# The Fourier branch's output map on half of the positions, in an encoder block on one Trainium2 core

## The chip, the core and the metric

The kernel runs on one core of one Trainium2 chip. The metric is the device time of one execution in microseconds; before the change it is 1738.92 us, the median of 3 runs (1738.01 to 1740.28). Engines are named as the profile does: PE is TensorE, DVE VectorE, ACT ScalarE, POOL GpSimd, SP SyncE, which here issues nearly all DMAs, in the order of its own queue.

## The reference

One encoder layer on two batches: a sample of 1024 tokens and a prompt of 256, each with 16 meta tokens in front (1040 and 272 positions), model width 1024. What the change touches is branch A and the merge:

```python
def fourier_mix(f):
    fg = f.astype(jnp.float32).reshape(b, l, N_FOURIER_GROUPS, FOURIER_GROUP)
    y = jnp.real(jnp.fft.fftn(fg, axes=(1, 3), norm='ortho'))
    return y.reshape(b, l, FOURIER_WIDTH).astype(f.dtype)
...
    a = bidirectional_gqa(q, k, v) @ w_attn_o
    fo = fourier_mix(f) @ w_four_o
    merged = g_attn * a + g_four * fo
    x = x + merged @ w_out
```

f has 4 groups of 128 channels. The real part of the 2-D transform is a sum of two products: cosine over positions with cosine over channels, less sine with sine. Over the L positions the cosine part is even (position l and L - l have the same value) and the sine part is odd (opposite sign). Over the 128 channels of a group it is likewise, so channels 0 to 64 determine the rest.

## The kernel before

All matrix products run in three passes: each float32 operand is split into a high part (a cast to float32r) and a low part (the operand less its high part), and `three` (L213) issues high x high, high x low and low x high (L218, L219, L220). The tokens are in three chunks, `CH_N` = 512, 512 (sample) and 256 (prompt).

The stages: norms and transposed activations; the Fourier branch (`fourier`, L485) with part of the gate products beside it; queries and keys; attention, whose gaps on PE are filled with the gate products of chunks 1 and 2 (`gate_gen`, L425, drawn by a Filler); the merge (`merge`, L969), first chunk 0, then chunks 1 and 2; the output projection `w_out`; and the SwiGLU, the largest part.

`fourier` computes the channel products, then the position products: for the sample positions 1 to 520 (260 columns a half), for the prompt positions 16 to 271 (256 columns). The results come in five kinds of rows: even channels (2 tiles of 128 rows, 32 or 64 channels a group), odd channels (2 tiles), and the 4 rows of k = 64. For the sample the other positions are mirrored copies (L636, L639). `store` (L576) writes all of it to DRAM, `f_d`, for all 1280 tokens, 512 rows.

`load_af` (L938) fetches the attention output (two parts, added at L964) and the Fourier result of a chunk and splits both: 4 + 4 k tiles of 128 rows. `merge` goes over 8 units of 128 output columns. For each unit `load` (L973) fetches the weights (`w_m`: attention and even/odd Fourier rows; `w_mb`: the mirrored Fourier rows) and the two gates of the chunk; `need` (L988) adds and subtracts the mirrored rows (L992, L993), splits the 1024 columns (ACT L202, POOL L203), and takes the sigmoids. Then each chunk has 4 k tiles x 3 matmuls for the attention and as many for the Fourier half; DVE multiplies each with its gate (L1036, L1037), adds (L1038), and the sum is split into M (L1040, L1041). SP fetches two units ahead.

SBUF is a set of equal slots; a tile's slot comes free when its last reader is done. Within the attention, the order on PE, ACT and DVE is the program's; elsewhere a scheduler sets the order of each engine when the program is built, and an engine then works in that order. So a DMA that waits in SP's queue holds all later ones.

Of the kernel before, what the change touches and what calls it, by code (L numbers as in the profile page):

```python
# [17 lines left out]
P = 128  # L18
# [18 lines left out]
# pairs of token tiles of the SwiGLU's products: the first three with 384 columns, the others with 256  # L37
# [18 lines left out]
SLOT = 1056  # L56
N_SLOTS = 27
# [58 lines left out]
class Slot:  # L116
# [57 lines left out]
class Kernel:  # L174
    def __init__(self, tc, nc, a, o, pools):
# [18 lines left out]
        self.f_d = [self.dram.tile([512, n], F32, name=f"f_d{i}") for i, n in enumerate(CH_N)]  # L194

# [17 lines left out]
    def three(self, out, pairs, first=True, last=True):  # L213
        """out += hi.hi + hi.lo + lo.hi over pairs of ((stationary hi, lo), (moving hi, lo))."""
# [7 lines left out]
    def rstd(self, ss, n, scale, eps, name):  # L222
        """(ss * scale + eps) ** -0.5 for n sums a partition."""
# [7 lines left out]
    def norm(self, x, out, g, rows=P, name=""):  # L231
        """out = x * rsqrt(mean(x^2) + eps) (* g) along the columns."""
# [16 lines left out]
    # hT of chunk c: k pairs a slot (c0, c1), three k a slot (c2 with the meta tokens behind)  # L249
# [22 lines left out]
    def transpose_pair(self, hs, t, off, ps, name, tag="tr"):  # L272
        """Two token tiles (slots, 1024 columns) into hT columns off .. off+256."""
# [12 lines left out]
    def gained(self, t, ks, lo, hi, pt):  # L286
        """hT columns lo .. hi of some k tiles from the transposed rows, times the gains of their features."""
# [137 lines left out]
    def gate_gen(self, chunks, lo_engine):  # L425
        """Gate logits of the chunks; while there is a self.later, what is not for TensorE is put into it."""
# [57 lines left out]

    def fourier(self, ps):  # L485
        nc, a, sl = self.nc, self.a, self.sl
        # even and odd parts over positions n <-> L - n
# [26 lines left out]
        # channels: U[n, k] for every n tile, cos from the even part, sin from the odd part  # L514
# [34 lines left out]
        for j, m in enumerate((P, 9)):  # L549
            nc.gpsimd.dma_start(tp[j][:m, :1024], a["pos_p"][j, :m])  # L550
# [37 lines left out]
        # prompt: positions 16.. unfolded
        ms = [P, 9]
        for kind, p in kinds:  # L590
            rows = 4 if kind == "4" else P
            pf = ps.tile([P, 512], F32, tag="mm", name=f"fp{kind}{p}")
            tb = 512 if kind == "o" else 0
            self.three(
                pf[:rows, :256],
                [
                    (u_of(kind, p, up, j, m), (tp[j][:m, tb : tb + 256], tp[j][:m, tb + 256 : tb + 512]))
# [4 lines left out]
            nc.vector.tensor_copy(st[:rows, :256], pf[:rows, :256])  # L602
            store(kind, p, st, self.f_d[2], 0, 256, 2)
# [3 lines left out]
        # sample: positions l = 1..520, the others mirrored  # L607
# [9 lines left out]
        for i, (kind, p) in enumerate(kinds):  # L617
# [5 lines left out]
            for half in range(2):  # L623
# [9 lines left out]
                sgn = -1.0 if kind == "o" else 1.0  # L633
                if half == 0:
                    nc.vector.tensor_copy(st[:rows, 0:245], pf[:rows, 15:260])
                    nc.scalar.mul(st[:rows, 764:1024], pf[:rows, 259::-1], sgn)  # L636
                else:
# [3 lines left out]
            for c in range(2):  # L641
                store(kind, p, st, self.f_d[c], c * 512, (c + 1) * 512, c)
# [1081 lines left out]
```

## Time and profile before

| | before |
|---|---|
| median of 3 runs | 1738.92 us |
| span of the profiled execution (first to last instruction) | 1737.8 us |
| what lies around the span, by the median | 1.1 us |
| granted clock of PE, mean | 0.997 |
| attention ends (last product with the values) | about 663.7 us |
| the merge's matmuls | 670.9 to 787.6 us |
| output projection, first to last matmul | 787.6 to 904 us |

The profile gives busy time by engine, a chain of work that ended last, groups of instructions by line and tile, tables by stretch of time, and the instructions in order of time with what ended the idle time before each. Times are from the start of the span. A matmul's duration includes its way through the array, so that matmuls overlap; the distance between two starts is what each costs. In a row such as `m<-afl,ml 128*128 128x512`, m is the tile written, the next names are the tiles read (a slot may still bear an older name), then come the stationary and the moving operand's shapes.

### The profile page before, as it was taken

How to read it: one execution, taken by the hardware profiler on the slowest of the kernel's cores; microseconds unless marked ns; L12 is line 12 of the kernel's file. 1: busy time of each engine (PE TensorE's matmuls, PEld its weight loads, DVE VectorE, ACT ScalarE, POOL GpSimd, SP SyncE). 2: the span in 40 equal slices, each digit the busy share in tenths (PEclk: the TensorE clock that was granted, in tenths of full speed). 3: DMA queues.
4: the chain of work that ended last, by engine and by line, in shares of the span. 5: the costliest groups of instructions: out<-in, count | busy, mean ns of one | idle time of the engine just before them, and what ended most of it. 6: DMA issues, size and time to landing. Idle time of an engine off the chain costs nothing.

```text
span 1737.8 us, 25952 instructions
## 1 busy us (share of the span) xinstructions
PE 1697.8 (98%) x9917; PEld 1511.1 (87%) x9917; DVE 1140.9 (66%) x2084; ACT 720.6 (41%) x1391; POOL 239.6 (14%) x239
## 2 busy tenths in 40 slices
PE   7999999999999999999999999999999999999997
PEld 6888879878888888788879999999999998888886
DVE  5424544568777776963379766676666668765685
ACT  6323333456666666531355322222222234444444
POOL 3001333210100103423343000000000000000002
PEclk9999999999999999999999999999999999999999
DMA  5144331322222229735451222222232237553434
GB/s 190 63 149 162 116 116 55 122 74 67 70 61 59 61 79 352 250 119 170 145 182 64 85 82 95 90 96 89 94 98 84 71 126 255 198 182 101 159 97 153
DMA packets 100292, 212.06 MB, mean 122 GB/s; under 512 B 10373, under 2 KB 46877, under 8 KB 100168
## 3 DMA queue, kind: packets, MB, share of 16 engines
q1 hardware_dynamic: 90952, 192.98, 33.2%
q10 hardware_dynamic: 7824, 12.53, 2.0%
q0 software_dynamic: 1392, 4.90, 0.9%
q8 instruction: 78, 1.28, 0.3%
q14 instruction: 46, 0.38, 0.1%
HBM read 151.05 MB, written 59.31 MB: 121 GB/s over the span
## 4 chain that ended last, share of the span: by engine, by line
PE 67%; DVE 7%; DMA 3%; issue 3%; ACT 1%; POOL 1%; SPq 0%; POOLq 0%; DVEq 0%; ACTq 0%
PE i L218 9%; PE i L220 9%; PE i L219 9%; PE o L220 5%; PE o L219 5%; PE o L218 5%; PE S L898 4%; PE pt L832 4%; PE g L218 2%; PE pv L852 2%; PE g L219 2%; PE g L220 2%; PE pv L853 2%; PE wo L220 2%; PE wo L219 2%
## 5 line engine op out<-in xcount | busy, mean ns | idle before, releaser
L1227 ACT CAST w<-wi 128x512 fp32r<-128x512 f32 x168 | 104.0, 621 | 274.0 <-PE i L220 218.0
L218 PE MATMUL i<-A,w 128*128 128x384 f32 x616 | 208.4, 338 | 3.0 <-ACT w L1227 2.6
L220 PE MATMUL i<-A,w 128*128 128x384 f32 x616 | 208.1, 338 | 2.3 <-POOL w L1229 2.3
L219 PE MATMUL i<-A,w 128*128 128x384 f32 x616 | 207.9, 338 | 0.0
L218 PE MATMUL i<-Ah,w 128*128 128x256 f32 x616 | 173.0, 281 | 1.6 <-DVE sc L1283 1.5
L220 PE MATMUL i<-Ah,w 128*128 128x256 f32 x616 | 173.2, 281 | 0.0
L219 PE MATMUL i<-Al,w 128*128 128x256 f32 x616 | 172.9, 281 | 0.0
L834 ACT CAST pT<-pt 128x512 fp32r<-128x512 f32 x156 | 90.7, 582 | 97.1 <-PE pt L832 94.3
L835 DVE TENSOR_TENSOR pT<-pt,pT 128x512 fp32r<-128x512 f32 x156 | 106.9, 686 | 34.2 <-ACT pT L834 33.0
L1229 DVE TENSOR_TENSOR w<-wi,w 128x512 fp32r<-128x512 f32 x154 | 105.3, 685 | 28.7 <-ACT w L1227 28.3
L903 DVE TENSOR_REDUCE sm<-S 128x1 f32<-128x1040 f32 (+1 forms) x80 | 86.5, 1082 | 50.7 <-PE S L898 47.4
L218 PEld LDWEIGHTS i<-A,w 128*128 128x128 f32 x616 | 116.5, 189 | 3.6 <-ACT w L1227 2.9
L220 PEld LDWEIGHTS i<-A,w 128*128 128x128 f32 x616 | 116.4, 189 | 3.2 <-POOL w L1229 3.2
L218 PEld LDWEIGHTS i<-Ah,w 128*128 128x128 f32 x616 | 116.0, 188 | 2.2 <-DVE sc L1283 1.7
L219 PEld LDWEIGHTS i<-A,w 128*128 128x128 f32 x616 | 116.3, 189 | 0.0
L219 PEld LDWEIGHTS i<-Al,w 128*128 128x128 f32 x616 | 116.2, 189 | 0.0
L220 PEld LDWEIGHTS i<-Ah,w 128*128 128x128 f32 x616 | 116.0, 188 | 0.0
L227 POOL TENSOR_SCALAR fin0r<-fin0ss 128x1 f32<-128x1 f32 x1 | 0.8, 788 | 755.8 <-ACT X L235 755.8
L910 ACT ACTIVATE p<-S,sm 128x1040 f32<-128x1040 f32 (+1 forms) x80 | 80.2, 1003 | 33.6 <-DVE sm L903 27.0
L832 PE MATMUL pt<-ident,p 128*128 128x128 f32 (+1 forms) x624 | 93.4, 272 | 0.0
L220 PE MATMUL o<-wfo,act 128*128 128x512 f32 (+1 forms) x212 | 82.1, 388 | 2.1 <-DVE act L1361 2.1
L219 PE MATMUL o<-wfo,act 128*128 128x512 f32 (+1 forms) x212 | 81.9, 386 | 0.0
(745 smaller groups left out, 4475.9 us busy)
## 6 DMA issues: line engine op xcount, KB each, us to landing
wi<-w_fi SPq DMA_DIRECT2D x48, 512.0 KB
wg<-w_g SPq DMA_DIRECT2D x32, 512.0 KB
act_d<-sc SPq DMA_DIRECT2D x77, 192.0 KB
act<-act_d SPq DMA_DIRECT2D x37, 320.0 KB
wfo<-w_fo SPq DMA_DIRECT2D x21, 512.0 KB
X<-act_d SPq DMA_DIRECT2D x31, 320.0 KB
act_d<-sc SPq DMA_DIRECT2D x77, 128.0 KB
gate<-gs ACTq DMA_DIRECT2D x32, 256.0 KB
```

Of the source, the lines that this page charges most:

```text
L218: mm(out, sh, mh, start=first and i == 0, stop=False)
L219: mm(out, sh, ml, start=False, stop=False)
L220: mm(out, slo, mh, start=False, stop=last and i == n - 1)
L832: nc.tensor.transpose(pt[:rows, h * P : (h + 1) * P], me.ps4[h][:, col : col + rows], self.ident[:])
L834: nc.scalar.copy(pT[:rows, :512], pt[:rows, :])
L835: nc.vector.tensor_tensor(pT[:rows, 512:1024], pt[:rows, :], f32(pT[:rows, :512]), op=ALU.subtract)
L852: nc.tensor.matmul(me.pv[:], vst, pT[:rows, :512], start=j == 0, stop=False)
L898: nc.tensor.matmul(S[:, base + lo : base + hi], hq, self.kT[seq][g][v][:, lo:hi], start=v == 0, stop=v == 1)
L903: nc.vector.tensor_reduce(nb, S[:, base : base + L], axis=AX.X, op=ALU.max, negate=True)
L910: self.last_exp = nc.scalar.activation(p, S[:, base : base + L], AF.Exp, bias=nb, accum_out=total)
L1227: nc.scalar.copy(w[:, :512], src)
L1229: eng.tensor_tensor(w[:, 512:1024], src, f32(w[:, :512]), op=ALU.subtract)
```

## The change

The map `w_four_o` is linear, so it can be applied before the mirror. For an even-channel part X and an odd-channel part Y at positions 1 to 520 (sample) and 1 to 136 (prompt), together NL = 656 columns, the output at position l is X + Y and at L - l it is X - Y. The change

- stores the position products for those 656 columns alone (`f_d` is one array of 516 rows: 4 x 128, and 4 for k = 64), without the mirrored copies;
- adds a stage `fourier_out` behind the gate products of chunks 1 and 2: 8 units of 128 output columns x 2 halves of HL = 328 columns x (even, odd), 6 matmuls each and one more of 68 rows for k = 64 (its high and low parts stacked at partitions 0, 32 and 64). ACT copies both results from PSUM, POOL forms the sums and the reversed differences, and SP stores them to DRAM, `fo_d`, six DMAs a unit;
- the merge keeps the attention's 4 k tiles. It loads `fo_d`, POOL multiplies it with its gate, and DVE adds it. The weights' low part moves from POOL to DVE.

The new stage's first loads are issued at the 15th of the 16 gate units.

```diff
+        self.f_d = self.dram.tile([516, NL], F32, name="f_d")
+        self.fo_d = [self.dram.tile([P, 1280], F32, name=f"fo_d{i}") for i in range(8)]
...
+            if then and i == 14:
+                next(then)
...
+        def store(kind, p, st, lo, n):
+            row = {"e": p * P, "o": 256 + p * P, "4": 512}[kind]
+            m = 4 if kind == "4" else P
+            nc.sync.dma_start(self.f_d[row : row + m, lo : lo + n], st[:m, :n])
...
-                if half == 0:
-                    nc.vector.tensor_copy(st[:rows, 0:245], pf[:rows, 15:260])
-                    nc.scalar.mul(st[:rows, 764:1024], pf[:rows, 259::-1], sgn)
-                else:
-                    nc.vector.tensor_copy(st[:rows, 245:505], pf[:rows, 0:260])
-                    nc.scalar.mul(st[:rows, 505:764], pf[:rows, 258::-1], sgn)
+                (nc.scalar.copy if half else nc.vector.tensor_copy)(st[:rows, b : b + 260], pf[:rows, :260])
...
+    def fourier_out(self):
...
+        def load(i):
+            if i < 8:
+                raws[i] = sl.get("wmf")
+                nc.sync.dma_start(raws[i][:, :512], a["w_mf"][i])
+                nc.sync.dma_start(raws[i][:, 512:1024], a["w_mb"][i])
+
+        def need(i):
...
+            vec(w[:, :256], w[:, :256], w[:, 512:768], op=ALU.add)
+            vec(w[:, 256:512], w[:, 768:1024], w[:, 256:512], op=ALU.subtract)
+            u = units[i] = sl.get("wmf2", F32R)
+            nc.scalar.copy(u[:, :512], w[:, :512])
+            vec(u[:, 512:1024], w[:, :512], f32(u[:, :512]), op=ALU.subtract)
...
+        def part(r):
+            h, l = sl.get("fh", F32R), sl.get("fl", F32R)
+            nc.scalar.copy(h[:, :NL], r[:, :NL])
+            nc.gpsimd.tensor_tensor(l[:, :NL], r[:, :NL], f32(h[:, :NL]), op=ALU.subtract)
...
+        def tail(r, t, n, lo):
+            for b in (0, 32, 64):
+                nc.scalar.copy(t[b : b + 4, :n], r[b : b + 4, :n])
+            x = slice(lo, lo + 4)
+            nc.gpsimd.tensor_tensor(t[x, :n], r[x, :n], f32(t[x, :n]), op=ALU.subtract)
...
+        for i in range(8):
+            for half in range(2):
+                c = slice(half * HL, (half + 1) * HL)
+                pp = []
+                for odd in range(2):
+                    pm = self.mm[0].tile([P, 512], F32, tag=self.mm[1], name=f"fo{i}{half}{odd}")
+                    if odd == 0:
+                        nc.tensor.matmul(
+                            pm[:, :HL], y64[:68, i * P : (i + 1) * P], x64[:68, c], start=True, stop=False
+                        )
+                    for k in range(2 * odd, 2 * odd + 2):
...
+                        self.three(
+                            pm[:, :HL], [(w, (fh[k][:, c], fl[k][:, c]))], odd == 1 and k == 2, k % 2 == 1
+                        )
+                    pp.append(pm)
+                if half == 0:
+                    do(lambda i=i: (need(i + 1), load(i + 2)))
+
+                def out(i=i, half=half, pp=pp):
+                    st, sd = sl.get("fst"), sl.get("fsd")
+                    nc.scalar.copy(st[:, :HL], pp[0][:, :HL])
+                    nc.scalar.copy(st[:, 512 : 512 + HL], pp[1][:, :HL])
+                    spans = [(1, HL, LS, 0, 0)]
+                    if half:
+                        spans = [(1 + HL, NLS - HL, LS, 0, 0), (1, NLP, LP, NLS - HL, SEQ_S)]
+                    for l, n, L, b, t0 in spans:
...
+                        nc.gpsimd.tensor_tensor(sd[:, b + skip : b + n], x[:, skip:], y[:, skip:], op=ALU.add)
+                        t = t0 + l + skip - N_META
+                        nc.sync.dma_start(self.fo_d[i][:, t : t + n - skip], sd[:, b + skip : b + n])
...
+                        nc.gpsimd.tensor_tensor(d, x[:, n - 1 :: -1], y[:, n - 1 :: -1], op=ALU.subtract)
+                        t = t0 + L - (l + n - 1) - N_META
+                        nc.sync.dma_start(self.fo_d[i][:, t : t + n], d)
...
-        pieces = [(srcs, j) for srcs in (self.a_d[c], [self.f_d[c]]) for j in range(4 // per)]
+        pieces = [(self.a_d[c], j) for j in range(4 // per)]
...
+            nc.sync.dma_start(wa[:, :512], a["w_ma"][i])
...
+                nc.sync.dma_start(fo[:, :n], self.fo_d[i][:, 512 * c : 512 * c + n])
...
+                nc.gpsimd.tensor_tensor(fo[:, :n], fo[:, :n], gt[:, n : 2 * n], op=ALU.mult)
...
-            nc.vector.tensor_tensor(wa[:, 512:768], wa[:, 512:768], wb[:, :256], op=ALU.add)
-            nc.vector.tensor_tensor(wa[:, 768:1024], wb[:, 256:512], wa[:, 768:1024], op=ALU.subtract)
-            hl = self.split(wa, 1024, "wm", None, "t")
+            hl = sl.get("wm2", F32R, "t")
+            nc.scalar.copy(hl[:, :512], wa[:, :512])
+            nc.vector.tensor_tensor(hl[:, 512:1024], wa[:, :512], f32(hl[:, :512]), op=ALU.subtract)
...
-                nc.vector.tensor_tensor(gt[:, :n], pp[0][:, :n], gt[:, :n], op=ALU.mult)
-                nc.vector.tensor_tensor(gt[:, n : 2 * n], pp[1][:, :n], gt[:, n : 2 * n], op=ALU.mult)
-                nc.vector.tensor_tensor(gt[:, :n], gt[:, :n], gt[:, n : 2 * n], op=ALU.add)
+                nc.vector.tensor_tensor(gt[:, :n], pm[:, :n], gt[:, :n], op=ALU.mult)
+                nc.vector.tensor_tensor(gt[:, :n], gt[:, :n], fo[:, :n], op=ALU.add)
...
-            gates = Filler(self.gate_gen([1, 2], self.nc.gpsimd))
+            fo = self.fourier_out()
+            gates = Filler(chain(self.gate_gen([1, 2], self.nc.gpsimd, fo), fo))
```

Three places in the order of the built program follow. First SP at the merge's chunk 0. Before, the loads of the third unit (wm and wmb are weights, gt the two gates) and of the fourth stand one behind the other:

```order
L977 DMA wm_6933<-w_m 128x1024
L978 DMA wmb_6934<-w_mb 128x512
L983 DMA gt_6937<-gate_0_77 128x512
L984 DMA gt_6937<-gate_0_101 128x512
L977 DMA wm_6977<-w_m 128x1024
L978 DMA wmb_6978<-w_mb 128x512
L983 DMA gt_6981<-gate_0_80 128x512
L984 DMA gt_6981<-gate_0_104 128x512
```

Now the third unit's loads (wm_7406 on) stand behind the last unit's six stores (fo_d_223 is unit 0, fo_d_230 unit 7; fsd is what POOL writes) and the loads of fo for the first two units:

```order
L1037 DMA fo_d_230<-fsd_7361 128x313
L1043 DMA fo_d_230<-fsd_7361 128x328
L1105 DMA fo_6845<-fo_d_223 128x512
L1037 DMA fo_d_230<-fsd_7384 128x192
L1043 DMA fo_d_230<-fsd_7384 128x191
L1037 DMA fo_d_230<-fsd_7384 128x121
L1043 DMA fo_d_230<-fsd_7384 128x135
L1105 DMA fo_6854<-fo_d_224 128x512
L1090 DMA wm_7406<-w_ma 128x512
L1095 DMA gt_7408<-gate_0_77 128x512
L1096 DMA gt_7408<-gate_0_101 128x512
L1105 DMA fo_7409<-fo_d_225 128x512
```

Each store waits for POOL, so the merge's loads have moved behind POOL's last difference.

Second, SP inside the new stage, which the program before hasn't got. The weights of unit 7 (wmf_7252) stand behind the stores of unit 4:

```order
L1037 DMA fo_d_227<-fsd_7222 128x192
L1043 DMA fo_d_227<-fsd_7222 128x191
L1037 DMA fo_d_227<-fsd_7222 128x121
L1043 DMA fo_d_227<-fsd_7222 128x135
L949 DMA wmf_7252<-w_mf 128x512
L950 DMA wmf_7252<-w_mb 128x512
```

Units 5 and 6 stand likewise, three units behind the stores ahead of them.

Third, POOL between the gates' weights and the merge. Before, it takes the low parts of the merge's weights, one a unit:

```order
L203 TENSOR_TENSOR wmh_6845<-wm_6836,wmh_6845 128x1024
L203 TENSOR_TENSOR wmh_6929<-wm_6849,wmh_6929 128x1024
L203 TENSOR_TENSOR ml_1074_6940<-wm_6933,ml_1074_6940 128x1024
L203 TENSOR_TENSOR wmh_6845<-wm_6977,wmh_6845 128x1024
L203 TENSOR_TENSOR ml_1074_6940<-wm_7020,ml_1074_6940 128x1024
```

Now 48 sums (L1035) and differences (L1041) stand there, six a unit, and behind them the products with the gates (L1112):

```order
L1035 TENSOR_TENSOR fsd_7361<-fst_7360 128x313
L1041 TENSOR_TENSOR fsd_7361<-fst_7360 128x328
L1035 TENSOR_TENSOR fsd_7384<-fst_7383 128x192
L1041 TENSOR_TENSOR fsd_7384<-fst_7383 128x191
L1035 TENSOR_TENSOR fsd_7384<-fst_7383 128x121
L1041 TENSOR_TENSOR fsd_7384<-fst_7383 128x135
L1112 TENSOR_TENSOR fo_6845<-fo_6845,gt_6844 128x512
L1112 TENSOR_TENSOR fo_6854<-fo_6854,gt_6853 128x512
```

POOL thus got the sums and differences and the gating, and lost the splits of the weights, which went to DVE.

More of the change, by code (lines that the diff above doesn't have):

```diff
@@ L56 @@
 SLOT = 1056
+NLS, NLP = 520, 136
+NL = NLS + NLP
+HL = NL // 2
 N_SLOTS = 27
@@ L423, with gate_gen @@
     FILL = {"s": 640, "p": 400, "end": 640, "drain": 900}
-    def gate_gen(self, chunks, lo_engine):
+    def gate_gen(self, chunks, lo_engine, then=None):
         nc, a, sl = self.nc, self.a, self.sl
@@ L592, in fourier @@
             pf = ps.tile([P, 512], F32, tag="mm", name=f"fp{kind}{p}")
[L593 removed]
+            tb = 2 * NLP if kind == "o" else 0
             self.three(
[L595 removed]
+                pf[:rows, :NLP],
                 [
[L597 removed]
+                    (u_of(kind, p, up, j, m), (tp[j][:m, tb : tb + NLP], tp[j][:m, tb + NLP : tb + 2 * NLP]))
                     for j, m in enumerate(ms)
@@ L601, in fourier @@
             st = self.small.tile([P, 512], F32, tag="stage", name=f"fps{kind}{p}")
-            nc.vector.tensor_copy(st[:rows, :256], pf[:rows, :256])
-            store(kind, p, st, self.f_d[2], 0, 256, 2)
+            nc.vector.tensor_copy(st[:rows, :NLP], pf[:rows, :NLP])
+            store(kind, p, st, NLS, NLP)
             yield 700
@@ L632, in fourier @@
                 )
[L633 to L639 removed]
+                (nc.scalar.copy if half else nc.vector.tensor_copy)(st[:rows, b : b + 260], pf[:rows, :260])
                 yield 1650
[L641 to L642 removed]
+            store(kind, p, st, 0, NLS)
             sl.put(st)
@@ L975, in load @@
                 return
-            wa, wb = sl.get("wm"), sl.get("wmb")
-            nc.sync.dma_start(wa[:, :1024], a["w_m"][i])
-            nc.sync.dma_start(wb[:, :512], a["w_mb"][i])
+            wa = sl.get("wm")
+            nc.sync.dma_start(wa[:, :512], a["w_ma"][i])
             gts = []
@@ L981, in load, with load_fo, gate_fo @@
                 n = CH_N[c]
-                gt = sl.get("gt")
+                gt, fo = sl.get("gt"), sl.get("fo")
                 nc.sync.dma_start(gt[:, :n], self.gates[i][c][:])
                 nc.sync.dma_start(gt[:, n : 2 * n], self.gates[8 + i][c][:])
-                gts.append(gt)
-            raws[i] = wa, wb, gts
+                gts.append((gt, fo))
+            raws[i] = wa, gts
+        def load_fo(i):
+            if i == 8:
+                return
+            for c, (gt, fo) in zip(chunks, units[i][1] if i in units else raws[i][1]):
+                n = CH_N[c]
+                nc.sync.dma_start(fo[:, :n], self.fo_d[i][:, 512 * c : 512 * c + n])
+        def gate_fo(i):
+            if i == 8:
+                return
+            for c, (gt, fo) in zip(chunks, units[i][1]):
+                n = CH_N[c]
+                nc.gpsimd.tensor_tensor(fo[:, :n], fo[:, :n], gt[:, n : 2 * n], op=ALU.mult)
         def need(i):
@@ L1011, in merge @@
         yield 0
+        load_fo(0)
+        load_fo(1)
+        gate_fo(0)
         for i in range(8):
             need(i + 1)
-            if i < 7:
+            gate_fo(i + 1)
+            if i < 6:
                 load(i + 2)
-            (wh, wl), gts = units.pop(i)
+                load_fo(i + 2)
+            hl, gts = units.pop(i)
             if i == 7:
                 next(then)
-            for c, gt in zip(chunks, gts):
+            for c, (gt, fo) in zip(chunks, gts):
                 n = CH_N[c]
@@ L1692, in layout @@
         "w_kv": rows(w[:, 512:768], 4),
-        "w_m": units(np.concatenate([A(w_attn_o)[0], fa])),
+        "w_ma": units(A(w_attn_o)[0]),
+        "w_mf": units(fa),
+        "w_64": w4[:, 64],
         "w_mb": units(fb),
```

90 lines of the change are left out of this document (62 added, 28 removed).

## The prediction

> **What bounds the kernel now.** I read the page first (busy time and the chain that ended last), then the merge's own instructions, then a table by stretch, and last the order in time of VectorE (DVE) and GpSimd (POOL) inside that stage.
>
> ```profile
> PE 1697.8 (98%) x9917; PEld 1511.1 (87%) x9917; DVE 1140.9 (66%) x2084; ACT 720.6 (41%) x1391; POOL 239.6 (14%) x239
> PE 67%; DVE 7%; DMA 3%; issue 3%; ACT 1%; POOL 1%; SPq 0%; POOLq 0%; DVEq 0%; ACTq 0%
> ```
>
> TensorE is busy 98% of the span and holds 67% of the chain that ended last: where it has fewer columns to stream, time can be won, if nothing else comes up in that stage. A column's price comes from a long stretch that TensorE alone bounds:
>
> ```profile
> 1000.00:1200.00 200.00, 200.00 (x1366) 200.00 (x1365) 134.43 (x265) 56.12 (x105) 0.00 (x0) 1.00 0.28 93
> L218 PE MATMUL i<-A,w 128*128 128x384 f32 x616 | 208.4, 338 | 3.0 <-ACT w L1227 2.6 <-DVE sc L1282 0.3
> L218 PE MATMUL i<-Ah,w 128*128 128x256 f32 x616 | 173.0, 281 | 1.6 <-DVE sc L1283 1.5
> ```
>
> 1366 matmuls in 200 us, 384 and 256 columns in equal numbers (616 each): 0.1464 us for 320 columns, 0.4575 ns a column. (The 338 and 281 ns of one overlap; they aren't the pace.) Now the merge, matmuls by the tile m, then the stretch it fills:
>
> ```profile
> 670.91 0.40 PE L218 MATMUL m<-wmh 128*128 128x512 f32 x1
> L220 PE MATMUL m<-afh,ml x82: 278/388/401, 685.2 to 787.4; 128*128 128x512 f32 x42, 128*128 128x256 f32 x40
> 671.00:787.00 116.00, 111.99 (x573) 93.99 (x572) 95.22 (x130) 52.72 (x67) 39.29 (x16) 1.00 0.64 226
> 705.00:735.00 30.00, 26.67 (x132) 21.65 (x131) 29.96 (x38) 14.97 (x19) 7.49 (x3) 1.00 0.61 209
> 675.00:680.00 5.00, 5.00 (x24) 4.05 (x23) 2.34 (x4) 2.80 (x4) 2.56 (x2) 1.00 1.04 395
> ```
>
> The columns are TensorE, its weight loads, DVE, ACT, POOL, clock, DMA share and GB/s. The merge runs from 670.9 to 787.6. Its 576 matmuls (8 units x 24 x chunks of 512, 512 and 256) are 245,760 columns, 112.4 us: 4.3 us are idle. But DVE is busy 95 of 116 us, and all of 705 to 735, where TensorE has its gaps; DMA is full at 395 GB/s early on. So TensorE bounds this stage with two others close behind. What makes DVE so long is seen here:
>
> ```profile
> 698.85 2.42 POOL L203 TENSOR_TENSOR ml<-wm,ml 128x1024 fp32r<-128x1024 f32 x1 [1.78 <-PE m L220]
> 701.23 2.85 POOL L203 TENSOR_TENSOR ml<-wm,mh 128x1024 fp32r<-128x1024 f32 x1
> 698.84 0.69 DVE L1037 TENSOR_TENSOR gt<-m,gt 128x512 f32<-128x512 f32 x1
> 701.74 3.42 DVE L964 TENSOR_TENSOR af<-af,af 128x1024 f32<-128x1024 f32 x1
> 708.49 1.21 DVE L964 TENSOR_TENSOR af<-af,af 128x1024 f32<-128x1024 f32 x1
> ```
>
> The same L964 takes 1.21 us alone and 3.42 beside POOL, ending only after POOL's 701.23 op does. L1037, with one input from PSUM, takes its usual 0.69 in the middle of a POOL op. So a DVE tensor_tensor with two SBUF inputs and a POOL tensor_tensor exclude each other: their times add up. [...]
>
> **The change part by part.** *TensorE.* The merge keeps 122,880 columns (56.2 us). The new stage "fo" has 8 units x 2 halves x 13 matmuls x 328 columns = 68,224 (31.2 us). Saved: 112.4 - 56.2 - 31.2 = **25.0 us**. The thirteenth matmul has 68 rows.
>
> ```profile
> 661.84 0.50 PE L853 MATMUL pv<-pT,v 128*128 128x512 f32 x1
> 662.27 0.50 PE L852 MATMUL pv<-pT,v 16*128 16x512 f32 x1
> 662.70 0.50 PE L219 MATMUL g<-hT1h,wgh 128*128 128x512 f32 x1
> 640.91 0.44 PE pt L832 x4
> 100.70 0.39 PE L531 MATMUL uep<-T,fep 128*128 128x65 f32 x2
> 100.92 0.39 PE L532 MATMUL uop<-T,fop 128*128 128x64 f32 x2
> ```
>
> Going from 128 rows to 16 and back costs 0.43 - 0.23 = 0.2 us each way. At that price 16 such matmuls cost 6.4 us, at that of a 128-row one nothing; I take nothing, because the bound below leaves TensorE that much slack, and keep 6.4 for the range. [...] The prompt's 30 position matmuls go from 256 to 136 columns: by the column 1.6 us saved; four 128-column transposes in 0.44 us say nothing saved; the 65-column products (two in 0.22 us, 1.7 ns a column) would say 3.4 us lost. I take nothing, the row nearest in width.
>
> *The fo stage's other engines.* Per unit POOL does six sums and differences of 313 to 121 columns, 1280 in all; DVE adds, subtracts and splits the weights.
>
> ```profile
> L444 POOL TENSOR_TENSOR wgl<-wg,wgh 128x512 fp32r<-128x512 f32 x28 | 36.1, 1291 | 253.6 <-ACT wgh L443 203.4 <-PE pt L832 49.5 <-issue 0.5
> L696 POOL TENSOR_TENSOR ropeA<-ropeA 128x128 f32<-128x128 f32 x10 | 4.9, 492 | 0.0
> L992 DVE TENSOR_TENSOR wm<-wm,wmb x16: 406/424/2631, 655.6 to 770.8; 128x256 f32<-128x256 f32 x16
> L1038 DVE TENSOR_TENSOR gt<-gt x24: 409/685/2393, 679.2 to 793.1; 128x512 f32<-128x512 f32 x16, 128x256 f32<-128x256 f32 x8
> ```
>
> Between 492 and 1291 ns POOL takes 2.08 ns a column and 0.22 us an op: 1280 x 2.08 + 6 x 0.22 = 4.0 us a unit. DVE takes 0.42 + 0.42 + 0.69 = 1.5. Since they add, a unit costs 5.4 us there against TensorE's 3.9. The first fo tile reaches POOL about 675.4 (matmuls from 670.9, the last operand parts about 1.5 us late, two ACT copies). POOL is then done at 675.4 + 8 x 4.02 + 7 x 1.52 = 675.4 + 42.8 = **718.2**, while TensorE alone would be done at 702.1. How far TensorE is held back is SyncE's (SP's) order: unit 7's weights queue behind unit 4's stores, which wait for POOL, at 718.2 - 3 x 5.35 = 702.2.
>
> ```profile
> 751.57 0.38 SPq L977 DMA_DIRECT2D wm<-w_m  x1
> 755.34 0.63 DVE L992 TENSOR_TENSOR wm<-wm,wmb 128x256 f32<-128x256 f32 x1 [3.48 <-DMA wm<-w_m]
> L443 ACT CAST wgh<-wg 128x512 fp32r<-128x512 f32 x60 | 36.1, 622 | 27.2 <-DMA wg<-w_g 17.4 <-PE f L219 4.8 <-DVE qs L775 1.5
> ```
>
> 512 KB came 3.8 us after issue; 256 KB, at 395 GB/s, 3.1. Then 0.42 + 0.42 + 0.62 (ACT) + 0.69, and about 1.0 of waiting for POOL ops: the two issues end near 702.6, so unit 7 starts at 708.9 and fo ends at **712.8**. Given back: 10.7.
>
> *The merge's start.* In SP's order the third unit's attention weights stand behind unit 7's last store (718.2) and one load: issue 718.7, landed 721.8, cast and subtracted 723.3. TensorE has finished the two units that it had by 712.8 + 5.6 = 718.4. Given back: 4.9.
>
> *Chunk 0, the other six units.* TensorE needs 12 x 0.234 = 2.8 us. DVE and POOL share three 512-column DVE ops (0.61 apart back to back) and POOL's 1.29: 3.1. Given back 1.8; end 741.9.
>
> *Chunks 1 and 2.* From 718.7 the queue brings 9.4 MB up to the attention operands of chunk 1, 24 us at 395 GB/s, landed about 744; add, cast, subtract (1.22 + 1.05 + 1.22) end at 747.5. Half of the operands are there earlier, so the first unit loses 4.2 us. Each of the 8 units then costs the shared pair 3 x 0.61 + 2 x 0.33 + 1.29 + 0.75 = 4.5 us against 4.2: 2.4. End: 741.9 + 4.2 + 33.6 + 2.4 = **782.1**, against 787.6: 5.5 us earlier.
>
> *Taken at nothing.* The mirrored copies that go from the Fourier stage (0.4 us each) lay beside a full TensorE, 100 of 100 us:
>
> ```profile
> 100.00:200.00 100.00, 100.00 (x532) 80.97 (x532) 39.13 (x73) 27.73 (x54) 19.68 (x25) 1.00 0.46 156
> 400.00:500.00 100.00, 100.00 (x611) 85.78 (x611) 78.91 (x117) 62.75 (x115) 10.31 (x8) 1.00 0.21 64
> ```
>
> ACT's new copies for the k = 64 rows (3 of 656 and 3 of 1024 columns, by L443's 622 ns for 512 some 6 us) stand among the attention's last casts; ACT idles 37 of 100 us there. Without that cover they cost up to 6. The output projection follows the merge without a gap, as now; it needs only the first tiles of M.
>
> **The sum.** 25.0 saved, 24.0 given back (10.7, 4.9, 1.8, 4.2, 2.4), and the 4.3 us idle of before is inside these: 5.3 to 5.5 us less. The profiled span was 1737.8, 1.1 below the median of 1738.92; 5.5 off the median is **1733.4 us**. A measurement of this kernel tells about 0.2% (3.5 us) from no change.
>
> **Rivals.** (1) *The shared pair isn't the bound:* if POOL's new ops are shorter, or DVE finds room between them, POOL ends near 675.4 + 32.2 = 707.6, TensorE at about 703.5, the third unit starts at 713, chunk 1 about 6 us after chunk 0: merge end near 771, 16.5 us saved, 1722. For it: DVE needs the pair for 1.5 of 5.4 us only. Against: L964's 3.42 us. (2) *The queue is worse than its bytes:* under a full DMA these loads land late:
>
> ```profile
> 685.63 6.46 DMA wm<-w_m
> ```
>
> 6.5 us from issue instead of 3.1 is 3.4 more wherever TensorE waits for a load (fo's last units, the third unit, chunk 1). Met at one or two of the three it makes 1736.8 to 1740.2, about 1738. (3) *Slower: POOL reads backwards.* The differences (654 of the 1280 columns) run through their inputs from the end. On DVE that costs nothing:
>
> ```profile
> L494 DVE TENSOR_TENSOR fe<-fT x4: 694/700/702, 68.3 to 85.0; 128x519 f32<-128x519 f32 x4
> ```
>
> 0.70 us for 519 columns with one input reversed. POOL has no such row. The differences are 2.0 us of a unit's 4.0; at twice that, 8 x 2.0 = 16 us more: 1749. It decides from 0.7 us a unit (a third more), where the gain is gone.
>
> **Chances.** Forecast (4 to 11 us less) 0.42; rival 1 (11 to 25 less) 0.18; rival 2 (within 3.5) 0.20; rival 3 0.20. So faster 0.60, same 0.20, slower 0.20. For 8 in 10 the range reaches to 1717, most of rival 1, with the 68-row bound inside, and to 1747, short of rival 3's price.
>
> **What would show it.** POOL's unit of six ops near 4.0 us, and DVE ops of fo at 2 to 3 times 0.42; fo's last matmul 10 us behind its column sum; a gap in the merge after its second unit, ended by a load; the last m matmul near 782. If fo's matmuls run at 0.15 us without gaps, the pair was no bound (rival 1). If POOL's differences cost more than its sums, rival 3. Wrong altogether would be a long wait at the attention's end, where six more ACT copies and SP's loads stand ahead of the last casts.

## The result and the profile after

The change makes the kernel slower: 1754.04 us (median of 4, 1753.64 to 1755.39) against 1738.47 for the kernel before (1738.01 to 1740.28), ratio 1.0085, 95% interval 1.0071 to 1.0099. Forecast were 1733.4 us and a range of 1717 to 1747; the time lies above it.

The page of the kernel after, engines' busy time and the chain that ended last:

```profile
PE 1691.1 (96%) x9837; PEld 1502.0 (86%) x9837; DVE 1121.4 (64%) x2058; ACT 730.9 (42%) x1431; POOL 273.1 (16%) x303
PE 49%; DVE 5%; DMA 2%; issue 2%; ACT 1%; POOL 1%; SPq 0%; POOLq 0%; ACTq 0%; DVEq 0%
```

PE has less to do and is busy a smaller share of a longer span: the columns saved came back as waits. (Busy time also contains matmuls at half clock, those of 512 columns 0.43 us apart instead of 0.23, below.) By stretch; the columns are length, PE, its weight loads, DVE, ACT, POOL, clock, DMA share and GB/s:

```profile
672.00:711.00 39.00, 34.58 (x210) 31.18 (x209) 17.01 (x22) 19.25 (x42) 32.07 (x45) 1.00 0.64 195
711.00:745.00 34.00, 26.79 (x99) 18.41 (x97) 20.38 (x27) 14.35 (x21) 12.96 (x13) 0.95 0.96 334
745.00:751.00 6.00, 0.00 (x0) 0.00 (x0) 4.10 (x6) 2.73 (x4) 0.00 (x0) 0.82 1.05 344
751.00:797.00 46.00, 40.15 (x192) 32.15 (x192) 38.33 (x55) 22.93 (x38) 19.14 (x16) 0.88 0.68 228
797.00:920.00 123.00, 119.14 (x526) 96.68 (x527) 51.75 (x66) 40.06 (x60) 44.33 (x31) 0.97 0.42 147
```

These are the Fourier stage fo, the merge's chunk 0, a gap with no matmul at all, chunks 1 and 2, and the output projection. No engine is full in chunk 0 (PE 26.8 of 34, DVE 20.4, POOL 13.0), though the DMA is (0.96). In chunks 1 and 2 PE and DVE are both near full (40.2 and 38.3 of 46), and PE's 40.2 contain half-clock matmuls. The places where PE waits, in order of time:

```profile
672.08 0.32 PE L1009 MATMUL fo<-pT,y 68*128 68x328 f32 x1
...
711.22 0.39 PE L225 MATMUL m<-afh,pT 128*128 128x512 f32 x1
...
719.83 0.50 PE L225 MATMUL m<-afh,pT 128*128 128x512 f32 x1 [2.90 <-ACT pT L1119]
...
744.12 0.39 PE L227 MATMUL m<-afh,ml 128*128 128x512 f32 x1
751.12 0.80 PE L225 MATMUL m<-ml,mh 128*128 128x512 f32 x1 [6.62 <-ACT ml L209]
753.41 0.80 PE L226 MATMUL m<-afl,mh 128*128 128x512 f32 x1 [1.50 <-DVE afl L210]
754.00 0.63 PE L227 MATMUL m<-ml,mh 128*128 128x512 f32 x1
754.43 0.63 PE L225 MATMUL m<-ml,mh 128*128 128x512 f32 x1
...
796.52 0.28 PE L227 MATMUL m<-afh,afl 128*128 128x256 f32 x1
799.40 1.15 PE L225 MATMUL wo<-woh,pT 128*128 128x512 f32 x3 [2.60 <-ACT woh L209]
...
920.25 0.40 PE L227 MATMUL wo<-woh,ml 128*128 128x512 f32 x1
```

In the kernel before, the merge's last matmul starts at 787.44, the projection's first at 787.55 with no wait, its last at 903.80:

```profile
787.55 0.39 PE L218 MATMUL wo<-woh,wmh 128*128 128x512 f32 x1
```

Against the prediction's times this makes:

| stretch | predicted | measured | more |
|---|---|---|---|
| up to the first fo matmul (merge's first before) | 670.9 | 672.1 | +1.2 |
| fo | 41.9 | 39.1 | -2.8 |
| merge, units 1 to 3 of chunk 0 (to 725.4) | 13.6 | 14.2 | +0.6 |
| units 4 to 8 | 15.5 | 18.9 | +3.4 |
| chunks 1 and 2, with the gap ahead of them | 40.2 | 52.3 | +12.1 |
| wait ahead of the projection | 0 | 2.8 | +2.8 |
| projection, first to last matmul | 116.2 | 120.8 | +4.6 |
| the rest | 834.0 | 833.4 | -0.6 |

The sum is +21.3, the distance of the spans (1753.6 against the forecast's 1732.3).

One period of chunk 0 in order of time, for DVE, ACT and POOL:

```profile
736.48 0.69 DVE L1168 TENSOR_TENSOR pT<-gt,pT 128x512 fp32r<-128x512 f32 x1 [0.76 <-ACT pT L1167]
737.09 0.68 DVE L1120 TENSOR_TENSOR ml<-wm,ml 128x512 fp32r<-128x512 f32 x1
737.69 0.68 DVE L1164 TENSOR_TENSOR gt<-m,gt 128x512 f32<-128x512 f32 x1
738.48 1.38 DVE L1165 TENSOR_TENSOR gt<-gt,fo 128x512 f32<-128x512 f32 x1
740.60 0.69 DVE L1168 TENSOR_TENSOR pT<-gt,pT 128x512 fp32r<-128x512 f32 x1 [0.74 <-ACT pT L1167]
...
736.35 0.61 ACT L1119 CAST ml<-wm 128x512 fp32r<-128x512 f32 x1
736.87 1.06 ACT L1124 ACTIVATE gt<-gt 128x1024 f32<-128x1024 f32 x1
739.94 0.62 ACT L1167 CAST pT<-gt 128x512 fp32r<-128x512 f32 x1 [2.02 <-DVE gt L1165]
...
738.01 1.30 POOL L1112 TENSOR_TENSOR fo<-fo,gt 128x512 f32<-128x512 f32 x1 [2.84 <-ACT gt L1124]
```

A unit takes 4.12 us where PE needs 2.81. DVE has four operations, 0.61 apart: 2.44. The addition (L1165) meets POOL's product, which runs from 738.01 to 739.31, and takes 1.38 instead of 0.69; call this the lock. Then DVE stands 0.76, because the next in its order (L1168) needs ACT's copy of that sum. Smaller distances make 0.25. The product is for the next unit, whose addition follows at 742.60: nobody needs it yet.

### The profile page after: what moved, and what is told of

Same layout as the page of the kernel before. It is cut to its first block, busy times and chain, and to the rows that moved or that the text cites. A ratio compares the mean times of both kernels' runs of the same rounds, so it can differ in the third digit from the quotient of the medians.

```text
span 1753.6 us, 26106 instructions
## 1 busy us (share of the span) xinstructions
PE 1691.1 (96%) x9837; PEld 1502.0 (86%) x9837; DVE 1121.4 (64%) x2058; ACT 730.9 (42%) x1431; POOL 273.1 (16%) x303
## 4 chain that ended last, share of the span: by engine, by line
PE 49%; DVE 5%; DMA 2%; issue 2%; ACT 1%; POOL 1%; SPq 0%; POOLq 0%; ACTq 0%; DVEq 0%
PE i L225 10%; PE i L227 10%; PE i L226 10%; PE o L227 5%; PE o L226 5%; PE o L225 5%; PE wo L226 2%; PE wo L227 2%; PE wo L225 2%; DMA wm<-w_ma 1%; DVE gt L1165 1%; DVE wi L1335 0%; DVE A L1295 0%; DVE h L1298 0%; POOL wol L210 0%
## 5 line engine op out<-in xcount | busy, mean ns | idle before, releaser
L227 PEld LDWEIGHTS i<-Ah,w 128*128 128x128 f32 x616 | 116.2, 189 | 0.0
L906 ACT ACTIVATE p<-S,sm 128x1040 f32<-128x1040 f32 (+1 forms) x80 | 80.2, 1002 | 33.7 <-DVE sm L899 27.0
```

The costliest lines, as they stand in the source:

```text
L227: mm(out, slo, mh, start=False, stop=last and i == n - 1)
L906: self.last_exp = nc.scalar.activation(p, S[:, base : base + L], AF.Exp, bias=nb, accum_out=total)
```

## Experiments

Each is an edit of the kernel after. Times without an interval are of one execution; the kernel before took 1737.03 us beside the first four, 1737.96 beside the next four and 1739.41 (median of 15, from 1736.62 to 1742.17) beside the last three. "Less" and "more" are against the kernel after (1754.04) unless another is named. One version, measured twice (both on VectorE, below), differed by 1.3 us, so that a microsecond or two says little by itself; the readings below come from the traces.

### The merge's product on VectorE

```diff
-                nc.gpsimd.tensor_tensor(fo[:, :n], fo[:, :n], gt[:, n : 2 * n], op=ALU.mult)
+                nc.vector.tensor_tensor(fo[:, :n], fo[:, :n], gt[:, n : 2 * n], op=ALU.mult)
```

> The merge's product of Fourier half and gate runs on VectorE instead of GpSimd; nothing else changes. Three theories for the 4.13 us a unit that chunk 0 takes between 725.4 and 744.4 (TensorE needs 2.81). (order) Each unit's weight cast and sigmoid stand on ScalarE behind the copy of the unit before last, and that copy waits for VectorE's addition, which GpSimd's 1.29 us product locks out: without GpSimd the addition takes 0.69 instead of 1.36, one product of 0.6 goes ahead of it on VectorE, off the loop most of the time: 3.4 to 3.7 us a unit, m's last matmul 3 to 6 us earlier than 796.5. (shared pair) VectorE and GpSimd exclude each other, so only the sum of their work counts: 1.29 + 4 x 0.61 = 3.7 becomes 5 x 0.61 = 3.05: 0.7 a unit less, the same to the eye. (DMA) the full DMA from 720 to 752 sets the pace: nothing changes, 4.1 a unit. So this run tells DMA from the other two, and not these from each other.

1736.83 us, 17.2 less than the kernel after. DVE in chunk 0:

```profile
732.84 0.69 DVE L1165 TENSOR_TENSOR gt<-gt,fo 128x512 f32<-128x512 f32 x1
733.45 0.68 DVE L1112 TENSOR_TENSOR fo<-fo,gt 128x512 f32<-128x512 f32 x1
734.28 0.69 DVE L1168 TENSOR_TENSOR pT<-gt,pT 128x512 fp32r<-128x512 f32 x1
734.89 0.68 DVE L1120 TENSOR_TENSOR ml<-wm,ml 128x512 fp32r<-128x512 f32 x1
735.49 0.68 DVE L1164 TENSOR_TENSOR gt<-m,gt 128x512 f32<-128x512 f32 x1
736.20 0.70 DVE L1165 TENSOR_TENSOR gt<-gt,fo 128x512 f32<-128x512 f32 x1
```

One operation more on DVE, and the period falls from 4.12 to 3.36: the product fills the time in which DVE waited for ACT's copy, and the addition isn't locked out. DMA as the bound falls: DMA was as full (0.95 of 709 to 738). The gain is larger than expected because it goes on. The merge's last matmul starts at 784.5 instead of 796.5, and the projection follows without a wait and lasts 117.2 instead of 120.8. Some 2.2 us of the gain aren't the edit's: the merge starts at 709.1 instead of 711.2, and no work ahead of it was changed.

### Fillers in the waits

```diff
+            if chunks[0] and i == 0:
+                self.busy(28)
...
+        if not apart:
+            self.busy(12)
```

`busy(n)` issues n matmuls of 512 columns on finished parts of M into a PSUM tile that is never read.

> Adds 28 matmuls of 512 columns whose result is never read just ahead of the merge's chunks 1 and 2 (6.55 us at full clock, into a wait of 6.62), and 12 ahead of the output projection (2.8 us, into a wait of 2.60); all operands are there. (clock follows waits) TensorE's granted clock is halved because TensorE had stood still: with the wait filled, the 19 matmuls from 751.1 to 762.4 take 0.23 instead of 0.43 us each, and the 16 or so behind 799.4 likewise: 3.6 + 3.1 saved, some 0.5 lost where the fillers last longer than the wait: 5 to 7 us shorter in all, 1747 to 1749. (clock has another cause: a power or time pattern) the slow stretch stays where it is or moves by the clock's own rhythm, and the time grows by 0 to 1 us.

1752.67 us. PE at the two places:

```profile
745.52 6.20 PE L1055 MATMUL warm<-afl,pT 128*128 128x512 f32 x26
752.17 0.49 PE L225 MATMUL m<-ml,mh 128*128 128x512 f32 x1 [0.46 <-ACT ml L209]
754.31 0.50 PE L226 MATMUL m<-afl,mh 128*128 128x512 f32 x1 [1.65 <-DVE afl L210]
754.65 0.39 PE L227 MATMUL m<-ml,mh 128*128 128x512 f32 x1
754.87 0.39 PE L225 MATMUL m<-ml,mh 128*128 128x512 f32 x1
...
800.98 0.39 PE L225 MATMUL wo<-woh,pT 128*128 128x512 f32 x1
801.21 0.39 PE L226 MATMUL wo<-wol,pT 128*128 128x512 f32 x1
```

Behind a filled wait matmuls start 0.23 us apart; behind the same wait unfilled 0.43. So the half clock follows PE's waits. The projection lasts 116.8 instead of 120.8; counted by matmuls 0.43 apart, some 3 of these 4.0 us are half clock, and the rest are two small waits that shrank. At chunk 1 nothing is won (752.17 to 797.54 is 45.4 us, as in the kernel after): DVE delivers operands no faster there, and behind the waits that are left (1.65, 1.34 and 0.47) matmuls start 0.43 apart again from 757 to 763.5. Fo lasted 2.0 longer in this run, and so the total shows only 1.4. Most of that is the half clock too:

```profile
691.87 0.51 PE L1009 MATMUL fo<-pT,y 68*128 68x328 f32 x1 [1.85 <-ACT fst L1026]
```

Behind this wait 13 matmuls start 0.27 apart. The kernel after has the same wait of 1.85 at 691.66, and its matmuls go on at 0.15.

### ScalarE's order

Here PE, ACT and DVE keep the order written, loads go one unit further ahead, and the weight cast and sigmoid of unit i + 2 stand ahead of unit i's copy.

```diff
+                if c == chunks[0] and i < 6:
+                    need(i + 2)
+                    gate_fo(i + 2)
                 nc.vector.tensor_tensor(gt[:, :n], pm[:, :n], gt[:, :n], op=ALU.mult)
...
+            with self.tc.manual_schedule(engines={E.PE, E.Activation, E.DVE}):
+                run_all(m0)
+                run_all(m12)
```

> In the merge the engines PE, ScalarE and VectorE keep the order written, each unit's weights and gates are loaded one unit further ahead, and the weight cast, sigmoid and gate product of unit i+2 stand ahead of unit i's copy on ScalarE instead of behind it. No work is added or taken away. (order) the loop over ScalarE's queue is cut: chunk 0's later units go from 4.13 to 3.1 to 3.7 us, and chunk 1's first operands, which stood behind chunk 0's last VectorE operations, are made when their data land (about 745): the gap of 7.0 us shrinks to 2 to 5: 5 to 10 us shorter, 1744 to 1749. (shared pair) same work on the same pair, 3.7 a unit: 0.4 a unit, 2 us shorter for chunk 0, nothing at the chunk's start. (DMA) nothing is won: the loads of chunk 0 take 1 MB a unit, 2.7 us at 390 GB/s, and TensorE then waits for landings named in the waits.

1763.87 us, 9.8 more. Chunk 0's units still take 4.13: the copy, the casts and the sigmoid came in another order by unit and in the same order in time, the product again met the addition. In chunks 1 and 2 the order written is worse than the scheduler's: PE waits 1.2 to 1.3 us in four units, and 5.3 ahead of the projection. The theory fell in this form.

### Loads further ahead

```diff
-                    do(lambda i=i: (need(i + 1), load(i + 2)))
+                    do(lambda i=i: (need(i + 1), load(i + 3)))
...
         load(1)
+        if not chunks[0]:
+            load(2)
         yield 0
```

> SyncE's order alone: the Fourier stage's weights are loaded one unit further ahead (ahead of the stores of the unit before), and the merge's third unit is loaded before the Fourier stage begins. (queue, as predicted) the waits of 2.0, 0.6 and 1.4 us in the Fourier stage, all ended by weights that stood behind stores, go, and the wait of 2.9 + 0.9 us for the merge's third unit with the half clock behind it (9 matmuls at +0.2): fo ends 3 to 5 us earlier than 711.2, the third unit begins at once, 6 to 10 us shorter by then, of which chunk 1's start, bound by DMA landings near 745, gives some back: 1745 to 1750. (shared pair) GpSimd was done at 714.0 and works 3.7 us a unit: the fo tiles then wait for PSUM or staging slots that GpSimd holds, and fo ends within 1 us of now.

1752.15 us, 1.9 less. A wait took the place of a wait, twice:

```profile
678.68 0.64 PE L226 MATMUL fo<-fl,afl 128*128 128x328 f32 x1 [5.66 <-POOL fl L982]
724.09 0.80 PE L225 MATMUL m<-afh,pT 128*128 128x512 f32 x1 [3.26 <-ACT pT L1120]
```

The third unit starts at once, as the queue theory has it, and the fourth, now the first behind the stores, waits 3.3. And fo, which starts at 667.9 here instead of 672.1, waits 5.7 for its last operand: in this build ACT casts that one behind the attention output's second half (673.38), whose sum waits 1.0 for its load.

Chunk 0's last units take 3.6 here, not 4.12, with the product on POOL as before:

```profile
740.99 0.69 DVE L1172 TENSOR_TENSOR pT<-gt,pT 128x512 fp32r<-128x512 f32 x1
742.39 1.45 DVE L1169 TENSOR_TENSOR gt<-gt,fo 128x512 f32<-128x512 f32 x1
```

The scheduler put the weights' subtraction (740.18) between the addition and the operation that needs ACT's copy, so that DVE doesn't wait for the copy, while the addition still meets the product (1.45). So without the wait, and with the lock still there, a unit takes 0.5 us less. This order came from the scheduler, and ACT's order changed with it, so it isn't a clean test.

### The product's sigmoid first

```diff
+            for c, (gt, fo) in zip(chunks, gts):
...
+                    nc.scalar.activation(gt[:, n : 2 * n], gt[:, n : 2 * n], AF.Sigmoid)
             hl = sl.get("wm2", F32R, "t")
...
-                    nc.scalar.activation(gt[:, : 2 * n], gt[:, : 2 * n], AF.Sigmoid)
+                    nc.scalar.activation(gt[:, :n], gt[:, :n], AF.Sigmoid)
...
+            with self.tc.manual_schedule(engines={E.Activation}):
+                run_all(m0)
+                run_all(m12)
```

> The product stays on GpSimd. In the merge the sigmoid is split, and ScalarE keeps the order written: a unit's copy, then the sigmoid of the next gates' Fourier half (which GpSimd's product waits for), then the weight cast, then the other half. ScalarE's work grows by about 0.1 us a unit. (lock loop) a unit lasts as long as the ring copy 0.52, cast 0.52, sigmoid 1.13, GpSimd's product 1.30, and the rest of VectorE's addition, locked out until that product ends, 0.55 and 0.1 on the way: 4.12 as measured. With the cast and half the sigmoid out of the ring it lasts 0.52 + 0.6 + 1.30 + 0.55 + 0.1 = 3.1, so that the sum of VectorE's own work, 3.1 to 3.5, takes over: chunk 0's units 5 to 8 at 3.1 to 3.5 us, m's end 4 to 8 us earlier than 796.5. (sum of the shared pair, as predicted) the work of the pair is unchanged: the pace stays where it is, 4.1, or grows by what ScalarE gains in work.

1751.45 us; chunk 0's units 4 to 8 still take 4.15 on average. The ring I had named isn't it:

```profile
740.08 0.69 DVE L1172 TENSOR_TENSOR pT<-gt,pT 128x512 fp32r<-128x512 f32 x1 [0.76 <-ACT pT L1171]
741.12 1.37 DVE L1124 TENSOR_TENSOR ml<-wm,ml 128x512 fp32r<-128x512 f32 x1 [0.35 <-ACT ml L1123]
...
744.58 0.69 DVE L1172 TENSOR_TENSOR pT<-gt,pT 128x512 fp32r<-128x512 f32 x1 [0.69 <-ACT pT L1171]
```

The product came earlier and locked out another operation, the weights' subtraction (1.37); the wait of 0.7 for the copy stayed. What the runs at 4.1 us a unit have in common is DVE's sequence with a wait for ACT in it.

### The Fourier stage's sums on VectorE, alone and with the product

```diff
-                        nc.gpsimd.tensor_tensor(sd[:, b + skip : b + n], x[:, skip:], y[:, skip:], op=ALU.add)
+                        nc.vector.tensor_tensor(sd[:, b + skip : b + n], x[:, skip:], y[:, skip:], op=ALU.add)
...
-                        nc.gpsimd.tensor_tensor(d, x[:, n - 1 :: -1], y[:, n - 1 :: -1], op=ALU.subtract)
+                        nc.vector.tensor_tensor(d, x[:, n - 1 :: -1], y[:, n - 1 :: -1], op=ALU.subtract)
```

> The Fourier stage's sums and differences run on VectorE instead of GpSimd; the merge's product stays on GpSimd. (pair and queue, as predicted) six operations of 121 to 328 columns take 1.9 to 2.1 us of VectorE a unit in place of 3.8 of GpSimd, with 1.5 of weights, 3.5 in all against TensorE's 3.9: the stores go out earlier, the weights behind them too, and fo lasts 33 to 35 us instead of 39.1; the merge's third unit waits less. The lock loop of the merge stays at 4.1 a unit: 4 to 7 us shorter in all than 1754.0. (rival: the fo stage is held by ScalarE's copies and weight casts, or by load landings, whatever engine sums) fo stays at 38 to 40 us.

1751.42 us, 2.6 less. Fo lasts 36.8 instead of 39.1, where 33 to 35 were expected: of the 7.9 us that it lasted beyond its columns, POOL and the queue behind it made 2.3. The merge stays at 4.1 a unit.

> Both on VectorE: the Fourier stage's sums and differences, and the merge's product. GpSimd has neither. If the two effects are independent, the gain of the product alone (17.2 us) and that of the sums alone add up, less what chunk 1's operands, bound by their landing and by VectorE's order, give back: 1730 to 1735. If VectorE becomes the bound of the merge (5 operations of 0.61 a unit, 3.1 to 3.4 against TensorE's 2.8), what the Fourier stage wins is kept all the same, since the merge's pace doesn't change.

1733.33 us: 20.7 less, where the two alone gave 17.2 and 2.6. Timed again, more often:

> The kernel with the Fourier stage's sums and differences and the merge's product on VectorE, as once before (1733.33 us), timed against the kernel before: 0.9965 to 0.998 of its time.

1734.63 us against 1739.41 for the kernel before, ratio 0.9972, interval 0.9961 to 0.9983. This version is faster than the kernel after, and by 0.3% than the kernel before. Its chunks 1 and 2:

```profile
744.00:783.00 39.00, 36.39 (x193) 30.16 (x193) 37.48 (x71) 23.87 (x38) 1.14 (x1) 0.95 0.88 292
```

DVE is busy 37.5 of 39 us there and is the bound (PE's columns are 33.7).

> As the run before, and two loads moved in SyncE's order: the merge's third unit is loaded before the Fourier stage, and chunk 1's operands are loaded and made one unit earlier. (queue) the third unit's wait of about 3 us behind the Fourier stage's stores goes, and with it a stretch at half clock if there is one; 2 to 4 us less than the run before. (a wait for a wait) the fourth unit's weights, now the first load behind the stores, are waited for instead, as when the loads were moved ahead with GpSimd summing (the third unit began at once, the fourth waited 3.4 us): 0 to 1 us less.

1741.86 us, 8.5 more than the version with both on VectorE (1733.33) without the loads moved. The third and the fourth unit wait for nothing now, so the stores' queue did cost them their wait. But fo's start pays again: it lasts 45.6, with waits of 3.4 and 1.4 in its first units for operands that ACT and POOL make later.

### VectorE's order, the product still on GpSimd

In chunk 0, DVE keeps an order in which nothing waits for ACT's copy: multiplication (i), weights' rest (i + 2), addition (i), result's rest (i - 1).

```diff
+                if not chunks[0] and i < 6:
+                    need(i + 2)
                 nc.vector.tensor_tensor(gt[:, :n], pm[:, :n], gt[:, :n], op=ALU.mult)
+                weight()
                 nc.vector.tensor_tensor(gt[:, :n], gt[:, :n], fo[:, :n], op=ALU.add)
...
-                nc.vector.tensor_tensor(ml[-1][:, b : b + n], gt[:, :n], f32(mh[-1][:, b : b + n]), op=ALU.subtract)
+                lows.append((ml[-1][:, b : b + n], mh[-1][:, b : b + n], gt, fo, n))
+                while len(lows) > (not chunks[0] and i < 7):
+                    low()
...
+            with self.tc.manual_schedule(engines={E.DVE}):
+                run_all(m0)
```

`weight` and `low` issue the two subtractions that `need` and the loop issued at once before. The edit also loads one unit further ahead, as the run with ScalarE's order did; there the pace stayed at 4.13.

> The product stays on GpSimd. In chunk 0 alone VectorE keeps an order written so that nothing it does waits for ScalarE's copy: product of PSUM and gate (i), rest of the weights (i+2), addition (i), rest of the result (i-1); weights and gates are loaded one unit further ahead for it; chunk 1's operands come ahead of unit 7's own operations. No work is added or taken away. (VectorE's own sequence) of chunk 0's 4.12 us a unit, 4 x 0.61 is VectorE's work, 0.67 is lost to GpSimd's lock, 0.76 to the wait for ScalarE's copy, 0.25 to smaller ones; without the wait it is 3.1 to 3.5, and the operands of chunk 1 start when they land, not behind chunk 0's tail: m's end 5 to 9 us earlier than 796.5. (sum of the shared pair) 4 x 0.61 + 1.29 = 3.7 a unit is the floor. (a ring through GpSimd's lock, whatever the order) the pace stays at 4.1, as it did in the two runs that changed ScalarE's order.

1748.63 us, 5.4 less. DVE, then POOL:

```profile
734.16 0.68 DVE L1191 TENSOR_TENSOR gt<-gt,fo 128x512 f32<-128x512 f32 x1
734.77 0.68 DVE L1139 TENSOR_TENSOR ml<-gt,afl 128x512 fp32r<-128x512 f32 x1
735.37 0.68 DVE L1189 TENSOR_TENSOR gt<-m,gt 128x512 f32<-128x512 f32 x1
736.13 1.02 DVE L1134 TENSOR_TENSOR wm<-wm,wm 128x512 fp32r<-128x512 f32 x1
737.07 0.68 DVE L1191 TENSOR_TENSOR gt<-gt,fo 128x512 f32<-128x512 f32 x1
...
734.86 1.74 POOL L1112 TENSOR_TENSOR fo<-fo,gt 128x512 f32<-128x512 f32 x1 [1.17 <-ACT gt L1126]
```

The same work on the same engines takes 2.9 to 3.2 us a unit on DVE (2.91 here), and PE runs the last units at 2.8, its own pace. DVE and POOL still exclude each other (736.13 takes 1.02 instead of 0.69, the product 1.74 instead of 1.29), but the multiplication, which reads PSUM, lies beside the product. So neither the sum of the pair's operations (4 x 0.61 + 1.29 = 3.7) nor the lock by itself held chunk 0 at 4.12. The order on VectorE did: in it the lock fell on the addition, and a wait followed. The gap ahead of chunk 1 falls from 7.0 to 4.5 as its operands come ahead of the last unit's tail, and m's last matmul starts at 789.3.

> The order of the run before, with the Fourier stage's sums and differences and the merge's product on VectorE. VectorE's work is 5 x 0.61 = 3.05 us a unit in chunk 0 and no wait is left: 3.0 to 3.1 instead of 3.36, and chunk 1's operands start 1 to 3 us earlier against chunk 0's end: 1729 to 1733, 0 to 4 us under the same without the order. If chunk 1's operands are bound by their landing (under a full DMA), chunk 1 begins no earlier and nothing is won.

1736.07 us, ratio 0.9976 (0.9966 to 0.9986): no better than without the order. Chunk 0's last units take 3.0 instead of 3.4, but the projection gets its wait back (0.7, then 1.0) and lasts 118.1 instead of 116.9.

## Why the prediction was wrong, point by point

**PE's columns: right.** 68-row matmuls cost no more than their columns where nothing is waited for (rows of one fo unit: starts 677.13, 677.28, 677.43, the middle one of 68 rows). The prompt's narrower matmuls, taken at nothing, saved 0.9 us, about half of what their columns would: from their first to the sample's first it is 6.6 us (105.40 to 112.00), before 7.5 (106.09 to 113.55). Another 0.7 had been won ahead of them, where nothing was changed. The last score matmul of the attention starts at 635.5 instead of 637.4. The attention's end gave that and 1.2 more back, in waits of 1.3 and 0.5 for the last casts and eight matmuls at half clock (0.43 us apart).

**The Fourier stage: close in time, and less so in cause.** POOL's six operations take 3.7 us a unit where they follow each other (684.78 to 688.44; predicted 4.0). Rival 3 falls: its reversed differences cost what the sums do.

```profile
684.78 0.86 POOL L1035 TENSOR_TENSOR fsd<-fst 128x313 f32<-128x313 f32 x1
685.59 0.89 POOL L1041 TENSOR_TENSOR fsd<-fst 128x328 f32<-128x328 f32 x1
```

Fo ended at 711.2 (predicted 712.8). The three waits of its later units (1.8, 0.4 and 1.3 us) end with weights that were loaded behind stores, the first by way of a copy that stands behind their cast on ACT. But POOL was done at 714.0 where 718.2 were predicted and had idle time in between, and with its sums on VectorE the stage got only 2.3 shorter. So the pair's sum, to which the prediction put all 10.7 us given back, explains the smaller part of the 7.9, and that the end came out near is partly luck.

**The third unit: right.** 5.8 lost where 4.9 were predicted; the last load behind the stores, as said, and 1.9 of the 5.8 are half clock (nine matmuls at 0.43), which the prediction didn't have. The waits themselves are 3.9.

**Chunk 0's pace is the step that failed first.** "Three 512-column DVE ops (0.61 apart back to back) and POOL's 1.29: 3.1" is the sum of the shared pair's work. As a floor it is about right: VectorE's order took 2.9 to 3.2. As a pace it supposes that each engine always has something to do. DVE works in a fixed order, and that order put an operation that needs ACT's copy right behind the addition that the copy needs. It took 4.12; 3.4 us lost beyond the prediction in units 4 to 8.

**Chunk 1's start is where that cost most: 13.9 us, predicted 4.2.** Of the 13.9, 6.8 are the gap, 3.6 half clock (19 matmuls, those of 512 columns 0.43 us apart) and 3.5 waits for the next operands. The loads were issued from 734.4 to 738.3, and the first addition (L1077) started only at 748.73, right behind the last unit's last operation on DVE. The prediction had it bound by the DMA. With VectorE's order and the product on GpSimd the loads were issued at the same times, and the addition ran at 741.98; the lines are of the kernel after and of that run:

```profile
748.73 1.22 DVE L1077 TENSOR_TENSOR af<-af,af 128x1024 f32<-128x1024 f32 x1
...
741.98 1.22 DVE L1077 TENSOR_TENSOR af<-af,af 128x1024 f32<-128x1024 f32 x1
```

With DVE ahead the gap shrank: 6.2 with the product on it, 4.5 with the order. What the half clock alone makes of the 13.9 isn't shown. What chunks 1 and 2 gave back after that, 4.7 instead of 2.4, goes with the product's place too: from their first to their last matmul it is 40.5 us with the product on VectorE, 45.4 in the kernel after.

**"The output projection follows the merge without a gap, as now": wrong by 7.4.** PE waited 2.8 for the cast of its first weights, which ACT does behind the merge's late copies; and the projection lasted 4.6 longer, some 3 of it at half clock and the rest in two small waits. A half clock after waits stood in the trace of before (matmuls of 384 columns 0.32 apart instead of 0.18 from 913 to 917, behind waits of 2.6 and 2.1), and the prediction left it out. In the kernel after, matmuls of 512 columns start 0.43 us apart at half clock instead of 0.23; the stretch from 721.4 to 724.9 follows waits of 2.9 and 0.9 us, the one at the attention's end (663.7 to 666.9) waits of 1.3 and 0.5. A wait's length doesn't decide by itself: the 3.06 us ahead of the third unit in the first experiment (717.83) were followed by the full clock (0.23). What decides stays open.

**Rivals.** The first asked whether the pair was a bound at all; for chunk 0 it wasn't, but time went the other way. The second, loads that land late, isn't what held chunk 0: DMA was full there, and in VectorE's order the same loads, under a DMA as full (0.96 of 712 to 740), served 2.8 us a unit. None of the three named an engine waiting inside its own order, and that was the slower side.

What stays open: fo's first unit waits between 0.4 and 1.7 us in versions that are written alike there, which moves totals by a microsecond or two; why wasn't tried.

## What to carry to other kernels

When a stage loses half of its matmuls, the chains that they covered become the pace: follow one unit around the engines' fixed orders, operation by operation, and add the waits, before a sum of busy times is taken for a time. A wait costs again behind it where the clock falls (3.6 us at chunk 1's start), and an engine that lags at the end of one stage delays the operands of the next. Moving work onto the busier engine can win, if it fills a wait there: one more operation on VectorE took some 15 us off.

## What the runs showed of the hardware

- VectorE and GpSimd delayed each other: beside GpSimd's product VectorE's addition took 1.38 us instead of 0.69 (the kernel after, 738.48), and beside VectorE's operations the product took 1.74 instead of 1.29 (VectorE's order, 734.86). The VectorE operation that reads PSUM ran beside that product in 0.68 (735.37).
- Behind waits of 1.3 and 0.5 us at the attention's end, over at 661.6, eight matmuls ran at half clock (0.43 us apart, up to 666.9). Fo's single wait of 1.85 us was followed by a dozen or so matmuls at half clock (0.27 apart) in two runs (the fillers', and VectorE's order with the product on GpSimd) and by none in the kernel after (0.15); a single wait of 3.06 us in the first experiment by none (0.23).
- With fillers the matmuls of chunks 1 and 2 ran at half clock from 757.1 to 763.5 instead of 751.1 to 762.5, and the two chunks took 45.4 us as in the kernel after, where VectorE is busy 38 of the stretch's 46 us. In the projection, which PE fills, the half clock cost some 3 us.
